# Two blocks of a transformer on one core: where low halves are kept, how head norms are summed, and the order ahead of the first expert

## The chip, the cores and the metric

The kernel runs on one core of a Trainium2 chip. The metric is the device time of one execution in microseconds (us). Engines are named as the profile names them: PE is TensorE's matmul, PEld its weight load, DVE is VectorE, ACT is ScalarE, POOL is GpSimd, SP is SyncE, which issues most of the transfers. A "q" behind an engine's name is its queue of DMA issues.

## The reference, cut to what matters

512 tokens of width 1024 (16 learned tokens are put ahead of them, 528 in all) go through two layers of a first block and one second block, all in float32.

```python
# first block, each of two layers
c_q = rmsnorm(c_q_raw, g_qa);  q = (c_q @ w_q_b).reshape(B, L, 8, 96)
k = concat([k_nope, broadcast(k_rope)]);  q, k = rmsnorm(q, g_qn), rmsnorm(k, g_kn)   # a norm per head
o = causal_block_attention(rope(q), rope(k), v)
# second block
p_diff = softmax(q1 k1) - lam * softmax(q2 k2)      # 8 heads, each with two halves of 64
merged = sigmoid(..) * attn_d + sigmoid(..) * lru_d
x = x + merged @ w_out
h2 = rms_norm(x);  logits of 4 groups and 16 experts; two experts of one group for each token
x = x + sum of silu(h2 @ w_gate) * (h2 @ w_up) @ w_down * weight
```

## The kernel before, in words

**Precision.** A large float32 product is made from three products in a rounded float32 format ("fp32r" in the trace): each operand is cast by ACT to a high half and DVE subtracts that from the original to get the low half (`split`, L139 to L147), and `mm3` (L149) adds high by high, low by high and high by low. Weights come by DMA as raw tiles of 128x1024, are split into `wh` and `wl` (L145, L146, a pool of 3), and feed `fm_steps` (L208): one step is one tile of 128 output features for all tokens, with `kt` input tiles and three matmuls for each. The steps are Python generators. Code elsewhere calls `next` on them, so that a step of matmuls stands between two steps of something that needs other engines: these are the fillers.

**Memory.** Pool `big` (L1695) has 30 slots under one tag, "A"; `pair` (L186) takes a slot for two tiles of 128x528. Tiles x2H/x2L (the normalised input of block 2), q, k, v, the gates' outputs, the heads' outputs o and the experts' raw weights all take turns in it. A tile that finds no free slot makes its writer wait for the last reader of the one whose slot it takes. Pool `med` holds smaller tiles with a few buffers to a name or a tag; tag "hl" there has two and is used, before attention 2, by the casts of LRU inputs and rope (L1022).

**Block 1, one layer** (`layer`, L378). c_kv and c_q are computed with the sums of squares on the way: ACT squares each output tile, POOL adds it up (`SquareSums.done`, L122 to L126) and `col_sums` (L370, its matmul is L374) multiplies by ones. `sums(10)` (L448) does so for c_q, whose factor `eq` is first read at L618. The inverse norm is broadcast (L452), k_rope follows (`kr` matmuls L467, `kpe` and `skr` to L490), then k and v. The q projection has six output tiles (`Q_TILES`), four for the part without rope and two for rope; `ev_q` (L531) evacuates each. The squares of q are to be summed by head: ACT makes the square (L535) and a rounded copy (L549), POOL the remainder (L550), and `q_sums` (L555, its matmul L559) multiplies both by a 0/1 table `heads` of 128x8, one tile behind. In layer 0 the tokens come in two column parts of 264, in layer 1 as one of 512. Behind it stand the z_mla steps and the k transposes (`k_steps`, L566), interleaved by hand at L599 to L622: the last `q_sums`, copies of the sums by ACT (L608), their transposes (L612), and the factor `r3q`.

**Block 2** (`block2`, L918). `attention2` (L1284) runs twice, b = 0 and 1, with four heads each. For a head, K and Q are transposed on PE (L1302) and cast by ACT (L1304). DVE makes the low halves (L1306), POOL copies halves across partitions (L1308, L1309). The tiles are KH, KL and QS, three slots of "A". KH[:, c] is the high half of K twice over, KL[:, c] its low half twice over; QS holds high and low of Q in one tile, so two matmuls of depth 128 (L1324, L1325) do what takes three otherwise. Four blocks of 128 queries follow: scores, maximum (L1326), exponential (L1328), difference, transposes (L1334), copy (L1336), product with v (L1338). After each block the generator yields, and the caller runs one filler step: for b = 1 eight steps of g_lru and then eight of g_attn (L1087 to L1096). At a head's end its output is normed, transposed (L1348) and split into a pair `o2`.

**Out of block 2 into the experts.** w_out_2 gives eight tiles `xo` (`ev_out`, L1156). Each is squared and summed, multiplied by the router's weights (`logits`, L1173), transposed into rows (`rows`, L1143) which are copied by ACT, scaled by POOL and stored to `hbuf` and `out` by SP. `finish` (logits, then rows) of a tile is held until the next tile is done; for the last, the order is sums, logits, sums, rows (L1182 to L1193). On the way SP issues loads of expert weights into slots of "A" (`prefetch`, L1110), 24 by the end. `routing` (L1398) takes a Sqrt (L1412), makes group and expert choices on DVE, ranks tokens by matmul (L1447, L1450), and `slots` (L1494) turns the ranks of some experts into a list of row numbers: a comparison `oh` on DVE for each of four token tiles (L1512), matmuls (L1507), a reduction `sl0s` (L1518). The weights' factors of the first lists follow in `factors` (L1520). `moe` (L1535) gathers an expert's 128 rows by an indirect DMA (L1550, POOL's queue), transposes them (L1560, `feature_major`), and runs gate, up and down of 16 experts; the last four of the first 28 loads go to ACT's queue (L1633).

The tile framework puts in all waits by itself and can reorder instructions of an engine within limits.

Of the kernel before, what the change touches and what calls it, by code (L numbers as in the profile page):

```python
# [20 lines left out]
P = 128  # L21
D = 1024
KD = D // P
# [111 lines left out]
class Builder:  # L135
# [107 lines left out]
    def const(self):  # L243
# [6 lines left out]
        nc.vector.memset(self.ones, 1.0)  # L250
        self.heads = cp.tile([P, len(Q_TILES), HEADS], F32R, name="heads")
        hh, lo = [cp.tile([P, len(Q_TILES), HEADS], F32, name=n) for n in ("hh", "hl")]
        for m, (rope, h) in enumerate(Q_TILES):
# [3 lines left out]
        G.tensor_scalar(hh, hh, 0.0, None, op0=ALU.is_le)  # L257
        G.tensor_tensor(self.heads, hh, lo, op=ALU.mult)
        self.fold = cp.tile([2 * ROPE, ROPE], F32, name="fold")
# [118 lines left out]
    def layer(self, l, pro, squares, w_ckv):  # L378
# [67 lines left out]
        if l == 0:  # L446
            rope_rows()
        eq = sums(10)  # L448
        V.scalar_tensor_tensor(eq, eq, 1.0 / 768, epsx, op0=ALU.mult, op1=ALU.add)
        V.tensor_scalar(eq, eq, EPS, None, op0=ALU.mult)  # L450
        inv_b = med.tile([P, T], F32, name="inv_b", bufs=1)
# [37 lines left out]
        skr = sm.tile([P, NT], F32, name="skr")  # L489
        V.tensor_reduce(skr, kpe, axis=AX.X, op=ALU.add)  # L490


# [38 lines left out]
        def ev_q(m, ps, c0, n):  # L531
            sl = slice(c0, c0 + n)
            if m not in live:
                live[m] = med.tile([P, T], F32, name="sq")
            S.activation(live[m][:, sl], ps, AF.Square)  # L535
            rope, h0 = Q_TILES[m]
            if rope:
                for i in range(4):
                    h = h0 + i
                    rows = slice(i * ROPE, (i + 1) * ROPE)  # L540
                    for f, r in enumerate((NOPE, QK)):
                        V.tensor_tensor(qT[h // 2][r:r + ROPE, h % 2, sl], ps[rows], self.TQ[f][rows, sl], op=ALU.mult)
            else:
                for e in range(2):
                    S.copy(qT[h0 // 2][:NOPE, e, sl], ps[e * NOPE:(e + 1) * NOPE])
            if c0 + n == T:
                sq = live.pop(m)[:, q0:]
                hl = [med.tile([P, T], F32R, name="z", bufs=4)[:, q0:] for w in "HL"]
                S.copy(hl[0], sq)  # L549
                nc.gpsimd.tensor_tensor(hl[1], sq, hl[0].bitcast(F32), op=ALU.subtract)  # L550
                if m:
                    q_sums(m - 1)
                live["hl", m] = hl

        def q_sums(m):  # L555
            hl = live.pop(("hl", m))
            for c, (a, w) in enumerate(q_cols):
                for i, t in enumerate(hl):
                    E.matmul(qs[c][:HEADS, :w], self.heads[:, m], t[:, a - q0:a - q0 + w],  # L559
                             start=m == 0 and i == 0, stop=m == len(Q_TILES) - 1 and i == 1)  # L560

# [38 lines left out]
        next(k_steps)  # L600
        next(z_steps)
        next(k_steps)
        q_sums(len(Q_TILES) - 1)
        sb = sm.tile([P, NT, HEADS], F32, name="sb")
        V.memset(sb[:, 0], 1.0)
        qss = med.tile([HEADS, T], F32, name="sq")
        for c, (a, m) in enumerate(q_cols):
            S.copy(qss[:, a:a + m], qs[c][:HEADS, :m])  # L608
        ps = self.psum()
        for j in q_tok:  # L610
# [9 lines left out]

        for _ in zip(z_steps, k_steps):
            pass  # L622
# [295 lines left out]
    def block2(self, xH, xL, squares, out):  # L918
# [181 lines left out]
        with ExitStack() as ctx:  # L1100
# [33 lines left out]
            for c in (0, SEQ):  # L1134
                nc.sync.dma_start(out[SEQ:SEQ + P, c:c + SEQ], zero)
            acc = self.psum()
            ssum = med.tile([P, SEQ], F32, name="ssum", bufs=1)
# [18 lines left out]
            def ev_out(m, ps, c0, n):  # L1156
# [14 lines left out]
                def logits():  # L1171
                    for j, (t0, w) in enumerate(TOK2):
                        E.matmul(acc[:, 20 * j:20 * j + 20], xo[:, t0:t0 + w], wr[:, m], start=m == 0 and j == 0,  # L1173
                                 stop=m == KD - 1, skip_group_check=True)

                def finish():
                    logits()
                    rows(m, xo)

                if m:  # L1180
                    held.pop()()
                prefetch(min(24, (11, 13, 14, 16, 18, 20, 26, 28)[m]))  # L1182
                if m < KD - 1:
                    held.append(finish)
                else:
                    square_sums(ssum)
                    logits()
                    square_sums(sq)
                    rows(m, xo)

            held = []
            self.fm(Weights(self, A["w_out_2"], 1024, 2), KD, 8, mH, mL, C0, ev_out)
            prefetch(24)  # L1193
            self.order = order
# [89 lines left out]
    def attention2(self, b, qkv, lneg, gs, out):  # L1284
# [9 lines left out]
        for hh in range(4):  # L1294
            h = 4 * b + hh
            KH = self.pair("kh2", F32R, (P, 2, SEQ))
            KL = self.pair("kl2", F32R, (P, 2, SEQ))
            QS = self.pair("q2", F32R, (P, 2, SEQ))
            for src, t2 in ((kt, KH), (qt, QS)):
                pt = self.ps_tr.tile([P, SEQ], F32, name="tr")  # L1300
                for j in range(4):
                    E.transpose(pt[:, j * P:(j + 1) * P], src[j][:, hh * P:(hh + 1) * P], self.ident)  # L1302
                for c, (own, other) in enumerate(halves):
                    S.copy(t2[own, c], pt[own])  # L1304
                    low = KL[own, c] if t2 is KH else t2[other, c]
                    V.tensor_tensor(low, pt[own], t2[own, c].bitcast(F32), op=ALU.subtract)  # L1306
                    if t2 is KH:
                        nc.gpsimd.tensor_copy(t2[other, c], t2[own, c])  # L1308
                        nc.gpsimd.tensor_copy(KL[other, c], KL[own, c])  # L1309
            po = self.ps_pv.tile([P, 4, P], F32, name="pv")  # L1310
            ot = med.tile([P, 4, P], F32, name="ot")
            so = sm.tile([P, 4], F32, name="so", bufs=2)
            for i in range(4):
# [7 lines left out]
                for c, (own, _) in enumerate(halves):  # L1321
                    c1 = slice(c, c + 1)
                    sc = self.ps_sc.tile([P, SEQ], F32, name="sc")
                    E.matmul(sc, QS[:, c, ts], KH[:, c], start=True, stop=False)  # L1324
                    E.matmul(sc, QS[:, c, ts], KL[:, c], start=False, stop=True)  # L1325
                    V.tensor_reduce(nm[:, c1], sc, axis=AX.X, op=ALU.max, negate=True)  # L1326
# [71 lines left out]
    def routing(self, acc, R):  # L1398
# [56 lines left out]
        V.tensor_tensor(rank_b.rearrange("p e j -> p j e"), ps4, ec_b, op=ALU.mult)  # L1455
        self.sl = self.slots(rank_b[:, 0:2], 2, "sl0", sm, False)
        ge, gw = sv("ge", 4, 4), sv("gw", 4)
# [23 lines left out]
        for q in range(3):  # L1481
            part = R["tok_b"][:, :, 3 + q * HX:3 + (q + 1) * HX]
            V.tensor_copy(part, fac)
            if q < 2:
                V.tensor_tensor(fac, fac, part, op=ALU.subtract)
        self.factors()
        self.cnti = sm.tile([P, 1], I32, name="cnti")
# [47 lines left out]
    def moe(self, out):  # L1535
        nc, A, tc = self.nc, self.A, self.tc
        V, S, E, G = nc.vector, nc.scalar, nc.tensor, nc.gpsimd
        with ExitStack() as ctx:
# [93 lines left out]
            W = [static_weights(e) for e in range(NE)]  # L1632
            xe = {e: gather(sl[e]) for e in range(2)}  # L1633
            for e, i in self.order[len(self.ahead):28]:
                self.ahead[e, i] = self.expert_weights(12 * e + i, queue=nc.scalar)
            x = feature_major(xe[0])
            sl += self.slots(self.rank_b[:, 2:4], 2, "sl2", self.route)
            nxt = {}
# [174 lines left out]
```

## Time and profile before

| | us |
|---|---|
| median of 3 runs (lowest, highest) | 1840.59 (1839.84, 1841.89) |
| the profiled execution | 1840.02 |
| its span in the profile | 1837.8 |
| PE busy in that span | 1742.7 (95 %) |

The span is what the profiler saw from the first to the last instruction; the execution's time has 2.2 us around it. Busy times of engines overlap. The timeline gives start and duration of instructions or of runs of equal ones ("x4" is a group of four, whose time goes from the first's start to the last's end); in square brackets stands the idle time before it and what ended it. An f32 matmul stands as two records, one of fp32r or bf16 as one. A window's line gives busy times, the mean clock granted to TensorE (1.00 is 2.4 GHz, 0.50 is 1.2 GHz), and the busy share and rate of the DMA engines.

### The profile page before, as it was taken

The page shows a single profiled execution, that of the slowest core. Times are in us where ns is not written, and L with a number is a line of the kernel's source. Part 1 is how long each engine was busy: PE and PEld are TensorE (multiplying, and loading weights), DVE is VectorE, ACT ScalarE, POOL GpSimd, SP SyncE. Part 2 cuts the span into 40 slices and gives each one's busy share as a digit, 9 for nine tenths or more (in the row PEclk, how much of TensorE's full clock was granted, in tenths as well). Part 3 has the DMA queues.
Part 4 walks back from the last instruction along what each step waited for, and adds up shares of the span by engine and source line. Part 5 has one row for each costly group of instructions (what it writes and reads, how often), then busy time and mean ns, then how long its engine had stood idle before and what let it go on. Part 6 is the DMA issues. An engine that isn't in the chain of part 4 may idle for free. (4 is left out here: it accounts for less than half of the span.)

```text
span 1837.8 us, 25780 instructions
## 1 busy us (share of the span) xinstructions
PE 1742.7 (95%) x9710; PEld 1469.6 (80%) x9710; DVE 1218.8 (66%) x2264; ACT 932.5 (51%) x1556; POOL 288.5 (16%) x261
## 2 busy tenths in 40 slices
PE   7989999999998999999998999999996997999997
PEld 7888899999976878788876777777874885888885
DVE  7575555456366455446689887577755528999996
ACT  5353244433344234433346666546645235888885
POOL 3122300001212320000213320011000031111111
PEclk9999999999999999999999999999998997999999
DMA  4222122123222122123422222122122588999992
GB/s 144 75 71 70 52 69 65 57 90 137 96 83 84 53 69 69 70 81 118 162 93 80 80 92 69 69 69 70 47 92 92 204 290 289 389 379 389 380 384 46
DMA packets 69091, 244.37 MB, mean 133 GB/s; under 512 B 10849, under 2 KB 20065, under 8 KB 57057
## 3 DMA queue, kind: packets, MB, share of 16 engines
q1 hardware_dynamic: 63776, 223.79, 33.8%
q0 software_dynamic: 4608, 16.78, 3.6%
q10 hardware_dynamic: 576, 2.10, 0.4%
q8 instruction: 78, 1.28, 0.3%
q14 instruction: 53, 0.43, 0.1%
HBM read 225.20 MB, written 17.37 MB: 132 GB/s over the span
## 5 line engine op out<-in xcount | busy, mean ns | idle before, releaser
L145 ACT CAST wh<-raw 128x1024 fp32r<-128x1024 f32 (+2 forms) x206 | 212.4, 1032 | 429.4 <-PE mm L152 358.3
L146 DVE TENSOR_TENSOR wl<-raw,wh 128x1024 fp32r<-128x1024 f32 (+2 forms) x206 | 255.0, 1239 | 107.8 <-ACT wh L145 106.3
L151 PE MATMUL mm<-xH,wh 128*128 128x264 f32 (+1 forms) x912 | 292.0, 321 | 12.9 <-ACT xH L361 8.7
L152 PE MATMUL mm<-xL,wh 128*128 128x264 f32 (+1 forms) x912 | 290.9, 320 | 0.7 <-DVE xL L362 0.7
L153 PE MATMUL mm<-xH,wl 128*128 128x264 f32 (+1 forms) x912 | 290.0, 318 | 0.0
L146 DVE TENSOR_TENSOR wl<-we,wh 128x1024 fp32r<-128x1024 f32 x192 | 227.7, 1219 | 14.9 <-ACT wh L145 12.5
L145 ACT CAST wh<-we 128x1024 fp32r<-128x1024 f32 x192 | 198.5, 1050 | 46.5 <-PE mm L153 32.0
L151 PEld LDWEIGHTS mm<-xH,wh 128*128 128x128 f32 x912 | 173.9, 191 | 25.3 <-ACT xH L361 8.7
L152 PEld LDWEIGHTS mm<-xL,wh 128*128 128x128 f32 x912 | 174.3, 191 | 11.8 <-DVE xL L362 1.5
L153 PEld LDWEIGHTS mm<-xH,wl 128*128 128x128 f32 x912 | 174.1, 191 | 10.3
L151 PE MATMUL mm<-wh,eH 128*128 128x512 f32 x256 | 104.8, 409 | 0.0
L153 PE MATMUL mm<-wh,eL 128*128 128x512 f32 x256 | 101.8, 398 | 0.0
L151 PE MATMUL mm<-x2H,wh 128*128 128x512 f32 x256 | 101.6, 397 | 0.0
L152 PE MATMUL mm<-wl,eH 128*128 128x512 f32 x256 | 101.5, 396 | 0.0
L153 PE MATMUL mm<-x2H,wl 128*128 128x512 f32 x256 | 101.0, 395 | 0.0
L152 PE MATMUL mm<-x2L,wh 128*128 128x512 f32 x256 | 100.9, 394 | 0.0
L126 POOL TENSOR_TENSOR z<-z,sq 128x528 f32<-128x528 f32 (+1 forms) x26 | 43.0, 1657 | 328.7 <-ACT sq L365 256.5
L151 PE MATMUL mm<-wh,x2H 128*128 128x512 f32 x192 | 77.3, 404 | 4.7 <-DVE rt__9409 L1264 2.7
L152 PE MATMUL mm<-wl,x2H 128*128 128x512 f32 x192 | 76.8, 400 | 0.0
L153 PE MATMUL mm<-wh,x2L 128*128 128x512 f32 x192 | 76.5, 402 | 0.0
L792 ACT ACTIVATE pr<-sc,bi,r3q 128x264 f32<-128x264 f32 (+3 forms) x80 | 46.6, 589 | 54.8 <-DVE bi L790 54.1
L152 PE MATMUL mm<-mgL,wh 128*128 128x264 f32 (+1 forms) x192 | 61.7, 321 | 0.0
(622 smaller groups left out, 4092.4 us busy)
## 6 DMA issues: line engine op xcount, KB each, us to landing
we<-in_w_moe SPq DMA_DIRECT2D x188, 512.0 KB
raw<-in_w_out SPq DMA_DIRECT2D x12, 1024.0 KB
raw<-in_w_g_mla SPq DMA_DIRECT2D x8, 1024.0 KB
raw<-in_w_g_pool SPq DMA_DIRECT2D x8, 1024.0 KB
raw<-in_w_c_q SPq DMA_DIRECT2D x6, 1024.0 KB
raw<-in_w_q_b SPq DMA_DIRECT2D x6, 768.0 KB
raw<-in_w_z_mla SPq DMA_DIRECT2D x4, 1024.0 KB
raw<-in_w_u_pool SPq DMA_DIRECT2D x4, 1024.0 KB
```

The lines of the kernel that those rows point to most:

```text
L126: self.kb.nc.gpsimd.tensor_tensor(self.sum[:, off:], self.sum[:, off:], sq[:, off:], op=ALU.add)
L145: nc.scalar.copy(H[:, :F], src)
L146: lo.tensor_tensor(L[:, :F], src, H[:, :F].bitcast(F32), op=ALU.subtract)
L151: mm(out, lH, rH, start=start, stop=False)
L152: mm(out, lH, rL, start=False, stop=False)
L153: mm(out, lL, rH, start=False, stop=stop)
L792: S.activation(pr[:, a:b, e], scs[q], AF.Exp, bias=bi[:, e:e + 1], scale=c, accum_out=su[:, e, q:q + 1])
```

## The change

1. *Low keys.* KL of attention 2 becomes two tiles of 128x512 under tag "hl" of `med`, not one slot of "A".
2. *Head sums.* `heads` becomes plain float32 and the squares of q are multiplied as they are: one f32 matmul replaces two fp32r ones, and the rounded copy and the remainder are not made.
3. *Row sums.* `sums(10)` and `eq` move behind kpe and skr. The last `q_sums` moves ahead of a k step, one z step is put between the copies and the transposes of the sums, and the rest is interleaved k first.
4. *Ahead of the first expert.* `warm` runs a Sqrt early. The last tile's logits and sums come ahead of the row copies of the last two tiles. The first list is made for expert 0 alone and its gather goes first; `factors`, the lists of experts 1 to 3 and the second gather follow. `prefetch` stops at 20, so that eight loads of the 28 go to ACT's queue, now behind `feature_major`.

```diff
@@ const, ev_q, q_sums
-        self.heads = cp.tile([P, len(Q_TILES), HEADS], F32R, name="heads")
+        self.heads = cp.tile([P, len(Q_TILES), HEADS], F32, name="heads")
...
-                live[m] = med.tile([P, T], F32, name="sq")
+                live[m] = med.tile([P, T], F32, name="z", bufs=4)
...
-                sq = live.pop(m)[:, q0:]
-                hl = [med.tile([P, T], F32R, name="z", bufs=4)[:, q0:] for w in "HL"]
-                S.copy(hl[0], sq)
-                nc.gpsimd.tensor_tensor(hl[1], sq, hl[0].bitcast(F32), op=ALU.subtract)
                 if m:
                     q_sums(m - 1)
-                live["hl", m] = hl
...
-            hl = live.pop(("hl", m))
+            sq = live.pop(m)
             for c, (a, w) in enumerate(q_cols):
-                for i, t in enumerate(hl):
-                    E.matmul(qs[c][:HEADS, :w], self.heads[:, m], t[:, a - q0:a - q0 + w],
-                             start=m == 0 and i == 0, stop=m == len(Q_TILES) - 1 and i == 1)
+                E.matmul(qs[c][:HEADS, :w], self.heads[:, m], sq[:, a:a + w], start=m == 0, stop=m == len(Q_TILES) - 1)
@@ layer
-        eq = sums(10)
-        V.scalar_tensor_tensor(eq, eq, 1.0 / 768, epsx, op0=ALU.mult, op1=ALU.add)
-        V.tensor_scalar(eq, eq, EPS, None, op0=ALU.mult)
...
         V.tensor_reduce(skr, kpe, axis=AX.X, op=ALU.add)
+        eq = sums(10)
+        V.scalar_tensor_tensor(eq, eq, 1.0 / 768, epsx, op0=ALU.mult, op1=ALU.add)
+        V.tensor_scalar(eq, eq, EPS, None, op0=ALU.mult)
...
         next(z_steps)
+        q_sums(len(Q_TILES) - 1)
         next(k_steps)
-        q_sums(len(Q_TILES) - 1)
...
             S.copy(qss[:, a:a + m], qs[c][:HEADS, :m])
+        next(z_steps)
...
-        for _ in zip(z_steps, k_steps):
+        for _ in zip(k_steps, z_steps):
+            pass
+        for _ in k_steps:
             pass
@@ attention2
-            KL = self.pair("kl2", F32R, (P, 2, SEQ))
+            KL = [med.tile([P, SEQ], F32R, name="kl2", tag="hl") for c in range(2)]
...
-                    low = KL[own, c] if t2 is KH else t2[other, c]
+                    low = KL[c][own] if t2 is KH else t2[other, c]
...
-                    E.matmul(sc, QS[:, c, ts], KL[:, c], start=False, stop=True)
+                    E.matmul(sc, QS[:, c, ts], KL[c], start=False, stop=True)
@@ block2, w_out_2
+            warm = route.tile([P, 1], F32, name="warm")
+            S.activation(warm, zero[:, :1], AF.Sqrt)
...
-                if m:
-                    held.pop()()
-                prefetch(min(24, (11, 13, 14, 16, 18, 20, 26, 28)[m]))
+                prefetch((11, 13, 14, 16, 18, 20, 20, 20)[m])
                 if m < KD - 1:
-                    held.append(finish)
+                    if m:
+                        held.pop()()
+                    held.append(lambda: (logits(), rows(m, xo)))
+                    if m == KD - 2:
+                        held[:] = [logits, partial(rows, m, xo)]
                 else:
+                    held[0]()
                     square_sums(ssum)
                     logits()
                     square_sums(sq)
+                    held[1]()
                     rows(m, xo)
...
-            prefetch(24)
@@ routing, moe
-        self.sl = self.slots(rank_b[:, 0:2], 2, "sl0", sm, False)
+        self.sl = self.slots(rank_b[:, 0:1], 1, "sl0", sm, False)
...
-        self.factors()
...
-            xe = {e: gather(sl[e]) for e in range(2)}
+            xe = {0: gather(sl[0])}
+            self.factors()
+            sl += self.slots(self.rank_b[:, 1:4], 3, "sl1", self.route)
+            xe[1] = gather(sl[1])
+            x = feature_major(xe[0])
             for e, i in self.order[len(self.ahead):28]:
                 self.ahead[e, i] = self.expert_weights(12 * e + i, queue=nc.scalar)
-            x = feature_major(xe[0])
-            sl += self.slots(self.rank_b[:, 2:4], 2, "sl2", self.route)
```

## Rows read from the trace of the kernel before

**Rows 1.** The page, part 1: the span and each engine's busy time.

```profile
span 1837.8 us, 25780 instructions
...
PE 1742.7 (95%) x9710; PEld 1469.6 (80%) x9710; DVE 1218.8 (66%) x2264; ACT 932.5 (51%) x1556; POOL 288.5 (16%) x261
```

**Rows 2.** Windows in attention 2: stretch, length, PE, PEld, DVE, ACT, POOL, clock, DMA.

```profile
1299.00:1331.00 32.00, 31.80 (x168) 25.43 (x167) 24.56 (x57) 19.48 (x44) 3.85 (x4) 1.00 0.19 66
1369.00:1411.00 42.00, 27.27 (x133) 19.05 (x132) 28.34 (x76) 23.89 (x60) 2.44 (x4) 0.88 0.08 26
1393.50:1403.80 10.30, 5.63 (x13) 3.52 (x14) 6.27 (x11) 3.60 (x8) 2.44 (x4) 0.50 0.00 0
```

**Rows 3.** The timeline from 1338 to 1370, PE and ACT, cut.

```profile
1340.39 0.58 ACT L1304 CAST kh<-tr 64x512 fp32r<-64x512 f32 x1
...
1342.49 0.63 PE L1302 MATMUL tr<-ident,qt 128*128 128x128 f32 x4
...
1368.73 0.39 PE L153 MATMUL mm<-x2H,wl 128*128 128x512 f32 x1
...
1369.30 0.58 ACT L1304 CAST q<-tr 64x512 fp32r<-64x512 f32 x1
```

**Rows 4.** The waits of PE: us in total, times, longest.

```profile
PE sc L559 <- POOL z L550: 8.0, 4, 4.3
...
PE pv L374 <- POOL z L126: 2.3, 2, 2.1
...
PE mm L612 <- ACT sq L608: 2.2, 2, 1.3
```

**Rows 5.** Windows of block 1 at the lower clock.

```profile
69.20:76.00 6.80, 6.63 (x30) 6.34 (x30) 1.96 (x10) 0.00 (x0) 0.00 (x0) 0.50 0.10 38
103.30:106.70 3.40, 3.40 (x18) 3.40 (x18) 3.09 (x11) 0.00 (x0) 0.00 (x0) 0.50 0.68 275
...
588.00:591.40 3.40, 3.40 (x9) 2.67 (x9) 2.31 (x12) 0.00 (x0) 0.00 (x0) 0.50 0.66 277
```

**Rows 6.** The timeline of PE in block 1: fp32r head sums and f32 scores.

```profile
117.94 0.65 PE L559 MATMUL sc<-z,heads 128*8 128x264 f32 x4
...
551.02 0.62 PE L559 MATMUL sc<-z,heads 128*8 128x512 f32 x2
...
649.57 1.05 PE L784 MATMUL sc<-kT,qT 128*128 128x264 f32 x4
```

**Rows 7.** The timeline from 1513 to 1533, all engines, cut.

```profile
1513.06 0.63 PE L1148 MATMUL tr<-ident,xo 128*128 128x128 f32 x4
...
1515.75 2.51 SPq L1153 DMA_DIRECT2D hbuf<-hr  x2
...
1516.55 1.28 ACT L1412 ACT_TABLE_LOAD   x1
...
1516.77 0.33 ACTq L1361 DMA_DIRECT2D we<-in_w_moe  x1
1517.85 0.26 ACT L1412 ACTIVATE v<-mm,eps 128x4 f32<-128x4 f32 x1
...
1522.85 1.43 DVE L1512 TENSOR_TENSOR oh<-iota_b,rank_b 128x256 bf16<-128x256 bf16 x4
...
1525.05 1.97 POOL L1550 DMA_INDIRECT xe<-hbuf,sl0s  x1 [7.18 <-DVE c L1469]
...
1528.86 0.51 PE L1507 MATMUL tr<-tok_b,oh 128*128 128x51 bf16 x8 [4.32 <-DVE tok_b L1483]
...
1531.64 1.73 PE L1560 MATMUL tr<-ident,xe 128*128 128x128 f32 x7 [2.27 <-DMA xe<-hbuf,sl0s]
```

**Rows 8.** Windows ahead of the first expert and within the experts.

```profile
1516.50:1531.60 15.10, 1.94 (x23) 1.34 (x22) 10.93 (x56) 4.22 (x7) 4.19 (x3) 0.50 0.99 336
1564.00:1794.00 230.00, 230.00 (x1097) 186.59 (x1096) 213.84 (x225) 196.64 (x229) 34.06 (x24) 1.00 1.03 382
```

**Rows 9.** The waits of SP's queue for a free slot: us in total, times, longest.

```profile
SPq L1361 <- DVE wl L146: 94.0, 80, 11.8
```

More of the change, by code (lines that the diff above doesn't have):

```diff
@@ L250, in const @@
         nc.vector.memset(self.ones, 1.0)
-        self.heads = cp.tile([P, len(Q_TILES), HEADS], F32R, name="heads")
-        hh, lo = [cp.tile([P, len(Q_TILES), HEADS], F32, name=n) for n in ("hh", "hl")]
+        self.heads = cp.tile([P, len(Q_TILES), HEADS], F32, name="heads")
+        hh, lo = self.heads, cp.tile([P, len(Q_TILES), HEADS], F32, name="hl")
         for m, (rope, h) in enumerate(Q_TILES):
@@ L257, in const @@
         G.tensor_scalar(hh, hh, 0.0, None, op0=ALU.is_le)
-        G.tensor_tensor(self.heads, hh, lo, op=ALU.mult)
+        G.tensor_tensor(hh, hh, lo, op=ALU.mult)
         self.fold = cp.tile([2 * ROPE, ROPE], F32, name="fold")
@@ L1174, in logits @@
                                  stop=m == KD - 1, skip_group_check=True)
-                def finish():
-                    logits()
-                    rows(m, xo)
-                if m:
-                    held.pop()()
-                prefetch(min(24, (11, 13, 14, 16, 18, 20, 26, 28)[m]))
-                if m < KD - 1:
-                    held.append(finish)
+                prefetch((11, 13, 14, 16, 18, 20, 20, 20)[m])
+                if m < KD - 1:
+                    if m:
[3 more added lines that the diff above has]
+                        held[:] = [logits, partial(rows, m, xo)]
                 else:
+                    held[0]()
                     square_sums(ssum)
@@ L1308, in attention2 @@
                         nc.gpsimd.tensor_copy(t2[other, c], t2[own, c])
-                        nc.gpsimd.tensor_copy(KL[other, c], KL[own, c])
+                        nc.gpsimd.tensor_copy(KL[c][other], low)
             po = self.ps_pv.tile([P, 4, P], F32, name="pv")
```

## The prediction

> **What bounds the kernel now.** I read the page's busy shares first. TensorE works 1742.7 us of a span of 1837.8, 95 percent, the next engine 66 percent [rows 1]. So a change that keeps the matmuls can win only what TensorE loses to waiting (some 95 us) and to its lower clock, and each edit has to be priced in the stretch where it lies. The second view was busy time by windows [rows 2]. From 1299 to 1331, while attention 2 computes two heads beside filler matmuls of the gates, TensorE works 31.80 of 32.00 us. From 1369 to 1411, where the last two heads run, it works 27.27 of 42.00, and within that, from 1393.5 to 1403.8, 5.63 of 10.30 us at a granted clock of 0.50, the lower level (1.2 GHz). The third view, the timeline of that place [rows 3], says why: the third head's K is transposed and cast by 1340.39, its Q is transposed at 1342.49, but ACT's first copy of Q starts only at 1369.30, just after the first matmul group of the last gate step ends (1368.73 plus 0.39). Between them nothing but gate matmuls run. ACT was not busy; the copy had no tile to write to. The code counts the same: pool "A" has 30 slots, and at that head 28 are taken (8 of x2H/x2L, 6 of q, k, v, 8 of the gates' output, 6 of finished heads), so KH and KL fill it and QS has to wait until the last gate step has read its x2 tile. The fillers meant for the last two heads are spent while TensorE waits for them.
>
> Fourth, the waits of TensorE [rows 4]: those that the change can touch are few, 8.0 us at L559, 2.3 at L374, 2.2 at L612. Fifth, windows behind these waits [rows 5]: four stretches at them run at 0.50, of which three are shown.
>
> **The change part by part.** Sums are made against the profiled execution, 1840.02 us (span 1837.8); the median of the runs shown, 1840.59, lies 0.57 higher, and I add that at the end.
>
> *KL in two "hl" tiles.* The third head then needs 28 + KH + QS = 30 slots, the fourth 29 + KH, and its QS takes the slot that kt leaves at the K transposes. So Q is copied behind its transposes and the gate steps spread over the heads, one beside each block. The ceiling is the idle time, 42.00 - 27.27 = 14.73 us, plus the clock's loss, half of 5.63 = 2.8: 17.5 us [rows 2]. The floor is 0, if the fillers then still run in a lump. I take 13: at the stretch's end the fourth head's own chain of softmax, transposes and output has no filler behind it. The "hl" tiles are shared with the casts before attention and turn over per head, and the next head's K low parts come well after the scores that read the last ones. That is covered by the filler beside a block; uncovered it would cost one wait of a few us a head, inside the range.
>
> *Plain f32 head sums.* Two f32r matmuls of a rounded and a remainder part become one f32 matmul, and ACT's cast and POOL's subtraction go. The 8.0 us of waits for POOL at L559 [rows 4] go with them, since ACT's square alone is then needed. The matmul costs more. Four f32r of 264 columns take 0.65, so a pair 0.33. By the records the scores at L784 are two matmuls, shown as x4: two of 264 columns take 1.05, one 0.525 [rows 6], and at 512 columns, by the columns, 1.02 against a pair's 0.62. That is +0.20 times 12 in layer 0 (six tiles, two column parts) and +0.40 times 6 in layer 1, +4.8 together; as bounds, 0 if all of it falls where TensorE idles, and 9.6 if it runs at the lower clock. I take 4.8, since TensorE is busy beside it. Two half-clock stretches of 3.40 us each (one a layer) lie at these waits, of which one stands in [rows 5]; without a stall they should run at full, which gives 1.7 each, 3.4. Net -8.0 - 3.4 + 4.8 = -6.6; range +1.6 (no clock gain, dear matmuls) to -11.4 (hidden matmuls).
>
> *Row sums moved.* The ten-column sum waits for POOL's squares, 2.3 us in two [rows 4]; behind kpe the squares are long there. After the wait TensorE runs 6.63 us at 0.50 [rows 5], of which 3.3 are loss. I take half of it, 1.7: -4.0, range 0 to -5.6. The two DVE operations on eq move with it and nothing reads eq before the keys' norms.
>
> *q_sums earlier, one z step ahead of the transposes.* L612 waits 2.2 for ACT's copies [rows 4]; the z step, matmuls of about 3.40 us of TensorE in the stretch after [rows 5], covers them. The half-clock stretch behind loses 1.7; I take half: -3.0, range 0 to -3.9.
>
> *Routing.* Here TensorE is nearly idle: 1.94 of 15.10 us from 1516.50 to 1531.60, DMA at 0.99 of its engines [rows 8]. What counts is when the gathered rows of expert 0 arrive, since from 1564 to 1794 TensorE works 230.00 of 230.00 us [rows 8], so a shift of its start carries to the end. The sums of squares now go ahead of both row copies (two groups of four transposes, 0.63 each [rows 7]), and the Sqrt's table, 1.28 us at 1516.55, is loaded long before by the warm activation. The Sqrt at 1517.85 moves some 2 us ahead; the list of one expert instead of two halves a part of the 1.43 us of "oh", so its list is there by about 1522, 3 us ahead of the gather's issue now (1525.05). But the row copies are later by the same edit: the last two hbuf stores, from 1515.75 to 1518.26, shift by about 1.5 us, and the gather reads what they wrote. So the gather can start between 1522 and 1524, and with 20 loads ahead instead of 24 fewer bytes stand in its way: xe's transposes begin now at 1531.64, 6.6 us behind the gather's issue [rows 7]. But an order stands against it: factors, which needs tok_b (the matmuls at 1528.86), and the lists of experts 1 to 3 now come ahead of expert 0's transposes. Moved 2 us ahead, those matmuls end at 1527.4 (0.51 long); the three lists, at one and a half times the width of the two now made, 1.5 times 1.43 or 2.1 us, end at 1529.5 at the earliest. In that order the transposes gain 2.1 us at most, without it up to 5. I take -3; range +1 (stores late) to -8 (all of it gained, and the gather's way shorter too).
>
> As to the table load, the row shows 1.28 us and the Sqrt 0.02 behind its end [rows 7]. The Trainium skill, "ScalarE: Activation LUTs", section What ACT_TABLE_LOAD costs, adds to a load of about 1.28 us a drain of about 1.38 for every switch of set; by it the sum would lie 1.4 us lower. The load agrees with the row, the drain isn't seen in it, and I stay with the row.
>
> *At nothing:* the casts and subtractions that go from ACT and POOL (51 and 16 percent busy [rows 1]), and the extra Sqrt load in the stage before, where TensorE's matmuls cover it.
>
> Sum: -13 - 6.6 - 4.0 - 3.0 - 3 = -29.6, so 1840.0 - 29.6 = 1810.4, and 1811 with the 0.57.
>
> **Rivals.** *The freed slot gives nothing* (0.17): the "hl" tiles turn into the new wait, or head 4's QS still waits, and the two heads stay bare. For it: buffers in this pool are all taken, so one more late release is enough. Against: the count of 30. It gives 1811 + 13 = 1824.
>
> *Small stalls only change their name* (0.08): at L559, L374 and L612 the next wait takes the place and the clock stays at 0.50 there, while f32 costs its 4.8. Then A, B and C together give +4.8 in place of -13.6: 1811 + 18.4, about 1829.
>
> *Both* (0.05): 1829 + 13 = 1842, no change.
>
> *Slower, by ACT's queue* (0.08). Eight loads instead of four are issued on ACT's queue, ahead of the next casts. On SP the same loads wait for free slots, 94.0 us in 80 waits, the longest 11.8 [rows 9]. If the slots aren't free, each of the eight holds ACT for such a wait w, and behind it queue the expert's casts, on which TensorE waits at once. Each costs w plus an issue of 0.33 [rows 7]; eight of them use up the 29.6 at w of 3.4 us. At 4.5 it is 8 times 4.83 = 38.6, and the time 1850. Against it: only 28 loads are ordered in all and the pool has 30 slots, with attention done.
>
> **How the numbers follow.** The forecast has 0.62: 1811, its own range, from the ends above, 1800 to 1823. The range goes to the second rival, 1800 to 1829, which leaves out the last two cases (0.13) and the forecast's tail. A difference of 0.2 percent, 3.7 us, is about the least that a measurement of this kernel can tell from none. Faster: 0.62 + 0.17 + 0.08 = 0.87; same 0.05; slower 0.08.
>
> **What would show it.** In the changed kernel's trace the first Q copy of the third head stands right behind its transposes, gate matmuls lie among the blocks of the last two heads, and no stretch at 0.50 is left there. L559 has 18 f32 matmuls (36 records) and no wait for POOL. No table load stands between the sums and the routing's Sqrt, and xe's transposes come some 3 us sooner after w_out_2's last matmul. The forecast is wrong if the Q copy still waits for the last gate step, if the stretches of [rows 5] stay at 0.50, or if ACT sits in front of its loads at the start of expert 0.

## The result and the profile after

The changed kernel takes 1810.75 us (median of four runs, 1807.85 to 1811.94), the kernel before in the same session 1841.24 (1839.84 to 1842.59): ratio 0.9832, interval 0.9815 to 0.9849, 30.5 us less. The forecast was 1811. The sum came out to within a microsecond, but its terms did not: several were off by 2 to 9 us, and they cancelled. That they cancelled so closely is luck. The profile of the changed kernel tells the terms apart. Its page, part 1, answers to [rows 1]: TensorE has 27 us less idle time and nearly the same work.

```profile
span 1808.2 us, 25732 instructions
...
PE 1740.5 (96%) x9706; PEld 1466.3 (81%) x9706; DVE 1215.0 (67%) x2264; ACT 925.2 (51%) x1545; POOL 264.8 (15%) x249
```

**The last two heads.** The timeline of the third head after the change, PE and ACT, answers to [rows 3].

```profile
1333.77 0.58 ACT L1302 CAST kh<-tr 64x512 fp32r<-64x512 f32 x1
...
1335.88 0.63 PE L1300 MATMUL tr<-ident,qt 128*128 128x128 f32 x4
1336.26 0.48 PE L152 MATMUL mm<-x2L,wh 128*128 128x512 f32 x1
...
1336.54 0.58 ACT L1302 CAST q<-tr 64x512 fp32r<-64x512 f32 x1 [1.44 <-PE tr L1300]
```

Q is copied 0.03 us behind its transposes (1335.88 plus 0.63), where the kernel before waited until 1369.30 [rows 3], and a gate matmul stands beside it. The whole stretch, from the K transposes of the third head to the output transposes of the fourth, as a window of the kernel before and of the one after (columns as in [rows 2]):

```profile
1331.05:1421.30 90.25, 75.03 (x358) 57.44 (x357) 48.96 (x121) 42.20 (x93) 6.85 (x17) 0.94 0.22 80
```

```profile
1324.44:1392.70 68.26, 67.92 (x352) 54.20 (x351) 48.06 (x121) 41.99 (x94) 7.90 (x17) 1.00 0.30 105
```

It is 22.0 us shorter. 14.9 of that is idle time (15.22 against 0.34). The other 7.1 lie in TensorE's own busy time, 75.03 against 67.92 for six records fewer.

**Block 1.** The waits of PE after the change, in answer to [rows 4]: L559 and L612 have none any more, L374 has one left.

```profile
PE pv L374 <- POOL z L126: 2.1, 1, 2.1
...
PE tr L1557 <- DMA xe<-hbuf,sl0s: 1.8, 1, 1.8
```

The f32 head sums in the timeline of PE, layer 0 and layer 1, in answer to [rows 6] (two records to a matmul):

```profile
101.03 1.06 PE L554 MATMUL sc<-z,heads 128*8 128x264 f32 x4
...
548.72 1.02 PE L554 MATMUL sc<-z,heads 128*8 128x512 f32 x2
```

They cost what was put in the sum: 1.06 for two of 264 columns (1.05 forecast from the scores) and 1.02 for one of 512. From the first w_q_b matmul to the first score, the windows of layer 0 and layer 1 in the kernel before, then after:

```profile
93.19:161.99 68.80, 61.79 (x486) 58.75 (x485) 50.21 (x115) 32.57 (x68) 11.62 (x6) 0.98 0.23 78
542.71:608.97 66.26, 59.10 (x264) 45.99 (x262) 42.75 (x87) 27.57 (x47) 12.66 (x6) 0.95 0.23 80
```

```profile
94.36:158.82 64.46, 63.22 (x487) 57.30 (x485) 47.04 (x115) 29.15 (x62) 0.00 (x0) 1.00 0.25 83
540.28:600.08 59.80, 59.61 (x264) 42.79 (x262) 42.16 (x87) 24.31 (x41) 0.00 (x0) 1.00 0.26 88
```

Layer 0 gives 4.34 us, layer 1 6.46, 10.8 together, and the clock, 0.98 and 0.95 before, is 1.00 in both. The row sums, on the other hand, were moved in the source, but in layer 0, where their wait is, not on the chip (in layer 1 they moved from 522.97, among the first `kr` matmuls, to 524.58, behind them). Around the sums of layer 0 the clock still falls (the first window of [rows 5]):

```profile
66.97:79.64 12.67, 10.62 (x62) 9.68 (x61) 3.68 (x14) 0.76 (x2) 2.00 (x1) 0.73 0.19 64
```

**Ahead of the first expert.** The last tile of w_out_2 is added up at 1512.45 in the kernel before:

```profile
1512.45 0.69 DVE L1160 TENSOR_TENSOR xo<-mm,xr 128x512 f32<-128x512 f32 x1 [4.76 <-PE mm L153]
```

and after the change the timeline, cut, answers to [rows 7]:

```profile
1484.82 0.69 DVE L1159 TENSOR_TENSOR xo<-mm,xr 128x512 f32<-128x512 f32 x1 [4.76 <-PE mm L153]
...
1486.33 0.63 PE L1147 MATMUL tr<-ident,xo 128*128 128x128 f32 x4
...
1487.61 0.63 PE L1147 MATMUL tr<-ident,xo 128*128 128x128 f32 x4
...
1488.08 0.95 PE L1167 MATMUL mm<-ones,sq 128*128 128x1 f32 x8
...
1489.07 0.26 ACT L1410 ACTIVATE v<-mm,eps 128x4 f32<-128x4 f32 x1 [0.16 <-PE mm L1167]
...
1496.29 1.97 POOL L1547 DMA_INDIRECT xe<-hbuf,sl0s  x1 [5.71 <-DVE c L1467]
...
1499.84 0.33 PE L1504 MATMUL tr<-tok_b,oh 128*128 128x51 bf16 x4 [4.05 <-DVE tok_b L1481]
...
1504.65 1.94 PE L1557 MATMUL tr<-ident,xe 128*128 128x128 f32 x8 [1.75 <-DMA xe<-hbuf,sl0s]
```

Counted from that addition, the Sqrt comes 4.25 us behind it (5.40 before: the table load is gone), the gather 11.47 (12.60 before), but expert 0's transposes 19.83 (19.19 before). What the earlier Sqrt gains, the gather gives back: 8.36 us from its issue to the transposes, 6.59 before [rows 7]. The shorter list itself gains nothing: from the Sqrt to the gather's issue it is 7.20 us before and 7.22 after. Its comparison `oh` takes 0.90 us instead of 1.43, but a copy ahead of it on DVE (`fac`, L1472) takes 0.81 instead of 0.16. Both groups of row transposes still stand ahead of the last sums, as before: the source says otherwise, but the framework orders each engine's instructions anew. Its order explains a second thing: all eight loads of ACT's queue are issued between 1451.94 and 1489.07, long before the experts, so the rival of a blocked ACT had nothing to stand on. The waits of SP for a slot, in answer to [rows 9]:

```profile
SPq L1359 <- DVE wl L146: 82.5, 73, 13.1
```

**The experts.** From the first expert's transposes to the end the changed kernel is shorter once more, which no step had foreseen. The transposes of successive experts in the timeline of PE of the kernel before, and after:

```profile
1593.21 1.03 PE L1560 MATMUL tr<-ident,xe 128*128 128x128 f32 x8
1612.01 1.04 PE L1560 MATMUL tr<-ident,xe 128*128 128x128 f32 x8
1630.06 1.03 PE L1560 MATMUL tr<-ident,xe 128*128 128x128 f32 x8
```

```profile
1565.54 1.03 PE L1557 MATMUL tr<-ident,xe 128*128 128x128 f32 x8
1584.15 1.03 PE L1557 MATMUL tr<-ident,xe 128*128 128x128 f32 x8
1602.05 1.03 PE L1557 MATMUL tr<-ident,xe 128*128 128x128 f32 x8
```

An expert takes 18.05 us before (1612.01 to 1630.06) and 17.90 after (1584.15 to 1602.05). One in four, with four lists made beside it, takes 18.80 and 18.61. From the first product (1533.58 and 1506.68) to the last matmul's end (1826.02 and 1796.17) that makes 292.4 and 289.5 us.

### The profile page after: what moved, and what is told of

Same layout as the page of the kernel before. It is cut to its first block, busy times and chain, and to the rows that moved or that the text cites. A ratio compares the mean times of both kernels' runs of the same rounds, so it can differ in the third digit from the quotient of the medians.

```text
span 1808.2 us, 25732 instructions
## 1 busy us (share of the span) xinstructions
PE 1740.5 (96%) x9706; PEld 1466.3 (81%) x9706; DVE 1215.0 (67%) x2264; ACT 925.2 (51%) x1545; POOL 264.8 (15%) x249
## 3 DMA queue, kind: packets, MB, share of 16 engines
q8 instruction: 78, 1.28, 0.3%
## 5 line engine op out<-in xcount | busy, mean ns | idle before, releaser
L151 PE MATMUL mm<-xH,wh 128*128 128x264 f32 (+1 forms) x912 | 292.3, 321 | 10.8 <-ACT xH L361 8.7
L152 PE MATMUL mm<-xL,wh 128*128 128x264 f32 (+1 forms) x912 | 291.4, 320 | 0.7 <-DVE xL L362 0.5
L151 PEld LDWEIGHTS mm<-xH,wh 128*128 128x128 f32 x912 | 174.7, 192 | 24.0 <-ACT xH L361 8.7
L152 PEld LDWEIGHTS mm<-xL,wh 128*128 128x128 f32 x912 | 174.4, 192 | 11.5 <-DVE xL L362 1.4
L151 PE MATMUL mm<-wh,eH 128*128 128x512 f32 x256 | 104.4, 408 | 0.0
L151 PE MATMUL mm<-x2H,wh 128*128 128x512 f32 x256 | 102.1, 399 | 0.0
L152 PE MATMUL mm<-x2L,wh 128*128 128x512 f32 x256 | 101.9, 398 | 0.0
L152 PE MATMUL mm<-wl,eH 128*128 128x512 f32 x256 | 101.0, 394 | 0.0
L151 PE MATMUL mm<-wh,x2H 128*128 128x512 f32 x192 | 77.5, 404 | 4.8 <-DVE rt__9342 L1262 2.8
L152 PE MATMUL mm<-wl,x2H 128*128 128x512 f32 x192 | 76.5, 399 | 0.0
L151 PE MATMUL mm<-mgH,wh 128*128 128x264 f32 (+1 forms) x192 | 61.7, 321 | 0.0
```

The costliest lines, as they stand in the source:

```text
L151: mm(out, lH, rH, start=start, stop=False)
L152: mm(out, lH, rL, start=False, stop=False)
```

## The experiments

**The low keys alone** (the kernel before with this edit):

```diff
-            KL = self.pair("kl2", F32R, (P, 2, SEQ))
+            KL = [med.tile([P, SEQ], F32R, name="kl2", tag="hl") for c in range(2)]
```

> Only the low keys moved into the two small tiles, all else as before. Theory: the slot decides, and alone it gives what the two traces differ by in the last two heads, 22.0 us, less 0.9 handed back in the next stage: about 1820. Rival (my forecast's own size): only the idle time and the clock inside 1369 to 1411 are won, 13 to 17.5 us: 1823 to 1828. Rival two: the gain needs the other edits too, since the framework orders everything anew: under 10 us.

Measured: 1821.47 us, ratio 0.989 (0.9874 to 0.9905), some 20 us less. The theory's number holds, and the second rival (under 10 us) falls. The interval in time ends at 1824 and so just touches the first rival (1823 to 1828); the trace settles it, since the stretch of the last two heads is 21.7 us shorter than the 90.25 before:

```profile
1333.33:1401.90 68.57, 68.23 (x354) 54.52 (x353) 48.02 (x121) 42.45 (x94) 7.90 (x17) 1.00 0.30 107
```

**All but the low keys** (the changed kernel with that edit undone):

> The changed kernel with the low keys back in a slot of the big pool. Theory: about 1811 + 21 = 1832, with the third head's Q copy again behind the last gate step. Rival: if the other edits carry the gain, it stays below 1820.

Measured: 1832.32 us, ratio 0.9951 (0.9936 to 0.9966), 21.6 above the changed kernel. Q's copy stands at 1362.01, its transposes at 1335.02. The edit is worth the same alone and on top of the others.

**29 slots:**

```diff
-            self.big = en(self.pool("big", 30, side="right"))
+            self.big = en(self.pool("big", 29, side="right"))
```

> The changed kernel with 29 slots in place of 30, the low keys still in small tiles. Theory: 28 taken + KH is 29, so the third head's Q copy waits for the gate steps once more and the gain of about 21 us goes, 1829 to 1835. Rival: if it is the low keys' place and not the count, the time stays within 4 us of 1811.

Measured: 1830.52 us, ratio 0.9936 (0.992 to 0.9951), 19.8 above the changed kernel. The third head's copies in the timeline of ACT:

```profile
1336.03 0.58 ACT L1302 CAST kh<-tr 64x512 fp32r<-64x512 f32 x1
...
1365.14 0.58 ACT L1302 CAST q<-tr 64x512 fp32r<-64x512 f32 x1
```

With the low keys in their small tiles, but one slot taken from the pool, Q waits 27 us behind its transposes (1338.14) again, and the stretch takes 90.51 us. It is the count of slots that decides, as the code's count of 28 said.

**The part ahead of the first expert alone** (warm, order of logits and rows, first list alone, 20 loads ahead, in the kernel before):

> Only the part ahead of the first expert (warm Sqrt, order of logits and rows, first list alone, 20 loads ahead). My forecast had -3 us. Theory from the two traces: the gather is issued 1.1 us sooner, its rows land no sooner because the loads of weights stand ahead of it in the DMA queues, and expert 0's transposes start within 1 us of before: 1839 to 1842. Rival: the 2.5 us that the experts are shorter in the changed kernel come from this part: 1838 or less, with experts 18.0 us apart or less.

Measured: 1838.48 us, ratio 0.9982 (0.9973 to 0.9991). Faster by 3 us, and yet not where the edits lie: from the row transposes of w_out_2's sixth tile to expert 0's it is 25.4 us in both (1506.22 to 1531.64 before, 1508.38 to 1533.76 here), and its experts stand closer:

```profile
1576.78 1.03 PE L1560 MATMUL tr<-ident,xe 128*128 128x128 f32 x8
1594.68 1.03 PE L1560 MATMUL tr<-ident,xe 128*128 128x128 f32 x8
```

The time lies between the two ranges that were expected, because a part of each came true: nothing from the routing, 17.90 us an expert. What made the experts closer was open.

**The head sums alone:**

```diff
-                for i, t in enumerate(hl):
-                    E.matmul(qs[c][:HEADS, :w], self.heads[:, m], t[:, a - q0:a - q0 + w],
+                E.matmul(qs[c][:HEADS, :w], self.heads[:, m], sq[:, a:a + w], start=m == 0, stop=m == len(Q_TILES) - 1)
```

> Only the plain f32 head sums. My forecast had -6.6 us. Theory: the four waits for POOL go and with them the half-clock stretch behind each, so from the first w_q_b matmul to the first score layer 0 gives 2 to 3 us and layer 1 some 3 to 4, 6 us together: 1835. Rival: the f32 matmuls' cost eats the gain, 1839 or more; or the whole 10.8 us that the two traces differ by in these two stretches come from here alone: 1831.

Measured: 1837.59 us, ratio 0.9974 (0.9964 to 0.9984). The two windows from w_q_b to the first score:

```profile
95.36:161.08 65.72, 63.33 (x486) 57.38 (x485) 47.42 (x115) 29.11 (x62) 0.00 (x0) 1.00 0.24 81
540.41:603.83 63.42, 61.24 (x264) 44.09 (x262) 42.44 (x87) 24.21 (x41) 0.00 (x0) 0.97 0.25 83
```

3.08 and 2.84 us less than before, 5.9 together, as the theory had it (layer 1 just under its 3 to 4). In layer 1 the clock comes back only in part with this edit alone: a wait of 2.0 us for DVE's copy of k (kT, L570) stands where the kernel before had 1.3 at L612. There a stall did change its name; in the changed kernel, with edit 3, it is gone.

**The last head sums earlier and a z step ahead of the transposes, alone:**

```diff
+        q_sums(len(Q_TILES) - 1)
         next(k_steps)
-        q_sums(len(Q_TILES) - 1)
...
+        next(z_steps)
         ps = self.psum()
```

> Only the last head sums earlier and one z step ahead of the transposes. My forecast had -3.0 us. Theory: the wait of 2.2 us at the transposes goes, with about half a stretch of lower clock: 1837 to 1839. Rival: the wait goes but the k transposes, now later, make the first scores wait: within 1 us of before.

Measured: 1838.39 us, ratio 0.998 (0.9969 to 0.999), with single runs from 1834.27 to 1842.43. The same windows:

```profile
95.67:163.06 67.39, 61.45 (x487) 58.68 (x485) 49.80 (x115) 32.63 (x68) 11.63 (x6) 0.97 0.24 79
545.38:608.26 62.88, 57.13 (x264) 44.68 (x262) 42.48 (x87) 27.72 (x47) 12.66 (x6) 0.97 0.25 84
```

1.41 and 3.38 less, 4.8 together. 5.9 and 4.8 make 10.7, and the changed kernel has 10.8: the two edits add up. With the second edit alone the wait at L612 is gone, the one at L559 stays (7.9 us).

**The experts: the tiles' place by 2 KB** (one early request of a tile in the kernel before):

```diff
             xe = {e: gather(sl[e]) for e in range(2)}
+            early = med.tile([P, 4, P], BF16, name="oh", bufs=2)
+            G.memset(early[:, 0, :1], 0.0)
```

> The kernel before with one more early buffer request in the experts' pool, so that eH, eL, hH and the lists' tiles lie at the addresses they have in the changed kernel (2 KB further on; one tiny memset is added), and no other edit. In all kernels with the edits ahead of the first expert the experts stand 17.9 us apart and without them 18.05, with the same instructions in the same order on each engine. Theory: the place of these tiles does it: 17.9 apart here as well, 1838 to 1839. Rival: it is the loads' order and queues or the lists of three: 18.05 apart, 1841 to 1842.

Measured: 1843.06 us, ratio 1.0003 (0.9994 to 1.0012). The theory, as it was put, falls: 18.06 us an expert.

```profile
1579.46 1.03 PE L1560 MATMUL tr<-ident,xe 128*128 128x128 f32 x8
1597.52 1.03 PE L1560 MATMUL tr<-ident,xe 128*128 128x128 f32 x8
```

But here the tiles were moved by 2048 bytes, and in the changed kernel, by the program's addresses, by an odd multiple of 32: warm, four bytes a partition, takes 32 in its pool and pushes all that lies behind it. So the next pair moved the tiles by 32 bytes, with one tiny copy on POOL and no other edit.

**Four bytes more in the kernel before, and four bytes more in the changed kernel:**

```diff
+            pad = route.tile([P, 1], F32, name="pad")
+            nc.gpsimd.tensor_copy(pad, zero[:, :1])
             acc = self.psum()
```

> The kernel before with one more tile of four bytes a partition in the pool of routing tiles (one tiny copy fills it), which moves eH, eL, hH, hL and every fourth wh by 32 bytes, as warm does in the changed kernel, and nothing else. Theory: it is these 32 bytes that make the matmuls of the experts closer: 17.9 us apart, the experts some 2.5 us shorter, 1839 to 1840. Rival: the loads' queues or the lists of three do it: 18.05 apart, 1842.

> The changed kernel with the same four bytes more, which puts these tiles 64 bytes, not 32, from where they were before. Theory: the experts go back to 18.05 us apart, 1813 to 1814. Rival: no change, 17.9 apart and 1811.

Measured: in the kernel before 1839.0 us, ratio 0.9985 (0.9977 to 0.9994), about 3 us faster; in the changed kernel 1814.82 us, ratio 0.9845 (0.9833 to 0.9858), 4 us slower in the median than without the pad. In the second pair the intervals overlap, and its trace has a slower start as well (last section), so the firm number is the experts' distance. Two experts each, the kernel before with the pad first, then the changed one with it:

```profile
1575.16 1.03 PE L1562 MATMUL tr<-ident,xe 128*128 128x128 f32 x8
1593.06 1.03 PE L1562 MATMUL tr<-ident,xe 128*128 128x128 f32 x8
```

```profile
1588.85 1.03 PE L1559 MATMUL tr<-ident,xe 128*128 128x128 f32 x8
1606.91 1.03 PE L1559 MATMUL tr<-ident,xe 128*128 128x128 f32 x8
```

17.90 and 18.06: the pad gives the kernel before the shorter experts and takes them from the changed one. The same two distances, to 0.02 us, part all fourteen traces: 18.05 in the six in whose programs eH lies at a multiple of 64 bytes, 17.90 in the eight where it lies 32 beyond one.

**The loads behind the first gather** (in the changed kernel):

```diff
+                            hold = xe[0] if len(parts) < 34 else None
...
+        if hold is not None:
+            self.nc.vector.tensor_copy(w[:, :1], hold[:, :1])
```

> The changed kernel with the six loads behind the 28 ordered ones held back until the first gather has landed (a one-column copy from its rows into each load's tile). Theory: the gather's rows come late because these loads stand ahead of them in the DMA queues; without them the rows are there in about 4 us after the issue instead of 8.4, and expert 0 starts up to 1.8 us sooner (TensorE's wait for the rows): about 1809. Rival: the gather takes its time for itself: no change, 1811. Third: the held loads come late for expert 1 and TensorE waits there: 1812 or more.

Measured: 1808.14 us, ratio 0.9817 (0.9803 to 0.983).

```profile
1497.79 1.97 POOL L1549 DMA_INDIRECT xe<-hbuf,sl0s  x1 [5.71 <-DVE c L1469]
...
1504.22 1.95 PE L1559 MATMUL tr<-ident,xe 128*128 128x128 f32 x8
```

From the gather's issue to the transposes 6.43 us, not 8.36, and TensorE no longer waits for the rows. By the DMA view the gather lands 5.2 us behind its issue, where it took 8.2 in the changed kernel; in five more traces with edit 4 and these loads not held it is 7.2 to 8.0, in the second one with them held (the last run below) 5.1. So the loads ahead of it did delay the gather, though the theory's 4 us was too little. The transposes now stand behind the lists of experts 1 to 3 on TensorE; 1.9 us is all that there was. In the medians this is not clear of the changed kernel's interval.

**The row sums pinned** (in the changed kernel):

```diff
-        eq = sums(10)
+        late = sm.tile([P, 1], F32, name="late")
+        V.tensor_scalar(late, skr[:, 1:2], 0.0, 1.0, op0=ALU.mult, op1=ALU.add)
+        eq = sums(10, late)
```

> The changed kernel with the ten-column sum made to stand behind skr by data (its column of ones is made from skr), since the move in the source left it in its place in layer 0, ahead of the broadcast of the inverse norm and with its wait of 2.1 us. Theory: the wait goes and part of the half-clock stretch behind it, -2 to -4: 1807 to 1809. Rival: the matmuls behind it wait for the same squares or for DVE in its place: within 1 us of 1811.

Measured: 1806.46 us, ratio 0.9807 (0.9794 to 0.9821), just under the theory's range. The place where the sum stood, in the timeline of PE of the changed kernel and of this one:

```profile
69.03 1.43 PE L374 MATMUL pv<-ones,z 128*128 128x1 f32 x10 [2.05 <-POOL z L126]
70.39 1.34 PE L346 MATMUL mm<-ident,trigq 128*128 128x128 f32 x4
```

```profile
67.67 1.04 PE L346 MATMUL mm<-ident,trigq 128*128 128x128 f32 x4 [1.31 <-DVE cqL L416]
68.64 2.17 PE L237 MATMUL mm<-ident,inv 16*128 16x16 f32 x10
```

The sum and its wait are gone from there, and a wait of 1.31 for the last c_q tile takes part of their place. From the first of the rope table's matmuls (L346, 65.16 and 64.55) to the first of the product that makes k and v (79.64 and 76.00) it is 14.48 against 11.45 us, 3.0 less. But the sum itself now stands in that product:

```profile
81.96 1.14 PE L374 MATMUL pv<-late,z 128*128 128x1 f32 x10
```

So the stage has to be taken to its end, the first w_q_b matmul (94.36 and 91.88): 29.20 against 27.33 us, 1.9 less. The medians differ by 4 us, with intervals that overlap a little; the 1.9 of the stage is the firmer number for this profile.

**Pinned and held together:**

> The pinned sum and the loads held behind the first gather together, in the changed kernel. Theory: the two lie in different stages and add up: 1.9 us from the gather and 2 to 4 from the sum, 1805 to 1807. Rival: what is won in block 1 is lost again in block 2, as some 2 us of the head sums' gain were: 1808 to 1809.

Measured: 1806.52 us, ratio 0.9806 (0.9793 to 0.9819), inside the theory's range, but no better in the median than the pinned sum alone (1806.46), so the medians do not show that the two add up. The stages do: from L346 to the first w_q_b matmul it is 25.73 us (66.49 to 92.22), 3.5 less than in the changed kernel, and from the last addition of w_out_2 to expert 0's transposes 18.16 (1480.69 to 1498.85), 1.7 less. The first differs from the 1.9 of the pinned sum alone by the clock only: from L346 to the product for k and v the granted clock was 1.00 here and 0.85 there, with the same instructions. The two kernels are the fastest of all that were run, 4 us below the changed kernel.

## Why the sum was right and its terms were not

| step | forecast | measured |
|---|---|---|
| low keys | -13 | -22.0 in the stretch |
| head sums | -6.6 | -5.9 |
| row sums moved | -4.0 | -0.3 (29.49 and 29.20 from L346 to w_q_b) |
| q_sums earlier, z step | -3.0 | -4.8 |
| routing | -3 | +0.6, inside the scatter |
| experts, 32 bytes | not foreseen | -2.9 |
| given back in block 2 | not foreseen | +2.2 ahead of the heads, +1 behind them |
| start of the program | not foreseen | +1.5 between these two profiles (L346 at 63.70 and 65.16) |
| the rest, most of it between the layers | not foreseen | +1.2 |

The measured terms add up to the difference of the two spans, 29.6 us, within rounding. Low keys, q_sums and the experts gave 13.7 more than was forecast; row sums, routing and head sums 8.0 less, and 5.9 were lost where no term stood. Nothing in the prediction made these sides meet, so the total is luck, and the mechanisms have to be judged one by one.

- **Low keys.** The mechanism held to the letter: the count of slots, Q's copy behind its transposes, the fillers beside the blocks. The rival that the freed slot gives nothing fell by the first run. The size, 13 for a measured 22.0, failed at two places. "At the stretch's end the fourth head's own chain ... has no filler behind it": only 0.34 us of idle time is left, since fillers and the first matmuls of w_attn_o were ordered into it. And the ceiling of 17.5 counted idle time and clock alone. In a bare stretch the same matmuls also stand as more busy time, since there is less to overlap; of the 7.1 us of busy time saved, 2.8 are the clock by [rows 2], about 1.4 the six records that fell behind the window (0.23 each by the distance of neighbours in the timeline, which came back as 1 us there: the output transposes are 28.6 us ahead, at 1420.64 and 1392.02, w_out_2's first matmul 27.6, at 1460.16 and 1432.52), and the rest, 2.9, is put down to this without a count of its own. (In the trace a matmul of 512 columns is 0.39 us long and the next starts 0.23 behind it; where none follows, the whole length counts.)
- **Head sums.** The mechanism was right: waits gone, matmuls at 1.02 to 1.06, clock back. The net was near, its two sides less so: with this edit alone TensorE's idle time in the two windows falls by 9.6 us (8.0 forecast) and its busy time rises by 3.7 (4.8 for the matmuls less 3.4 for the clock, 1.4, forecast).
- **Row sums.** Wrong, and for a reason that the prediction did not list: the edit did not do what it says. Moved in the source, the sum stayed in its place in layer 0. Where it was made to move, the stage gave 1.9 us with a part of the clock's loss left and 3.5 without it, against 4.0 forecast: the size was near, and the step that failed is that the move in the source was taken for one on the engine.
- **q_sums and the z step.** Right, sized too small: in layer 1 alone 3.4 us, wait and half-clock stretch together.
- **Routing.** The bound by order (a gain of 2.1 at most) was the nearer one, and even that was used up: the list won nothing, the sums did not go ahead of the row copies, and in this profile the gather lost 1.8 us behind loads in the DMA queues. The loss of 0.6 is no finding either. From the last addition to expert 0's transposes it is 19.19 to 20.26 us in six traces without edit 4 (19.19 the kernel before) and 19.00 to 19.83 in six with it and nothing held (19.83 the changed kernel). So the part is worth nothing that two profiles can tell. The Sqrt came 1.15 us sooner, which is as far as the last sums let it: they end 4.28 us behind the addition before and 4.21 after. So this move does not tell a price of 1.28 from a dearer one. The trace before does: ACT's copy ends 0.01 us ahead of the load (1515.95 plus 0.59) and the Sqrt starts 0.02 behind it [rows 7], so staying with the row was right. The Trainium skill, "ScalarE: Activation LUTs", section What ACT_TABLE_LOAD costs, has 2.66 with a drain, and no run here shows the drain.
- **What came besides.** In block 2 the first score of layer 1 is 8.9 us ahead (608.97 and 600.08), but the third group of head transposes of attention 2 only 6.7 (1128.26 and 1121.54). Part of it shows in two windows of the LRU, the kernel before and after, with the same stalls and another clock:

```profile
1010.00:1030.00 20.00, 16.73 (x66) 13.27 (x66) 19.73 (x33) 11.47 (x17) 9.52 (x8) 0.91 0.14 53
```

```profile
1002.00:1022.00 20.00, 16.91 (x62) 13.36 (x63) 19.19 (x33) 10.58 (x16) 9.33 (x7) 0.83 0.16 53
```

The slower rival, a blocked ACT, did not occur, and neither did the one in which small stalls only change their name: at L559 and L612 nothing took the place in the changed kernel.

- **The range.** The prediction says that its range, 1800 to 1823, follows from the ends of the parts. Added up, these ends are -46.4 and +2.6 us, so 1794 to 1843; the narrower range was a choice. The measured time lies in both.

## What to carry to other kernels

Count the slots of a shared pool at the point where a stall begins: one tile too many cost 20 us here, far from any engine's limit, and a run with one slot less shows it at once. A move in the source is not a move on the engine when a scheduler orders the instructions; look in the new trace where the moved one stands, and pin it by data if it has to move. And when an edit touches several stages, compare the traces stage by stage: a right total can be made of wrong terms.

## What the runs showed of the hardware that was not expected

**32 bytes.** A tile of four bytes changes the experts by 0.15 us of 18.05 (0.8 percent) each, with the same instructions in the same order on TensorE and VectorE and a granted clock of 1.00 in both. By the addresses of the programs eH, eL, hH, hL and every fourth wh lie at a multiple of 64 bytes in the slower kernels and 32 beyond one in the faster ones, while the other wh and wl lie 32 beyond one in all. Which of these tiles decides, and whether it is their place against the moving operand's, was not tried. The traces give a hint: behind an L152, whose stationary wl has the same place in all kernels and whose moving operand is eH, the next matmul starts 0.232 us later in three slower kernels and 0.230 in three faster ones (means of some 110 each), so the stationary tile's place is not all of it.

**The same stall, three clocks.** From 32 to 44 us, behind a stall of 1.9 to 2.1 us (L151 waits for `cqL`) that these kernels share, the granted clock was 1.00, 0.86 or 0.72, in the kernel before, the one with the low keys alone and the changed one with the pad in turn:

```profile
32.00:44.00 12.00, 10.09 (x85) 9.98 (x84) 9.04 (x42) 4.54 (x10) 2.08 (x1) 1.00 0.04 14
```

```profile
32.00:44.00 12.00, 10.13 (x73) 10.03 (x72) 8.33 (x39) 4.05 (x10) 2.09 (x1) 0.86 0.05 14
```

```profile
32.00:44.00 12.00, 9.87 (x62) 9.77 (x62) 8.10 (x45) 4.19 (x10) 0.00 (x0) 0.72 0.05 14
```

The edit of the second kernel lies in attention 2, a thousand microseconds later, so it is not the cause; the changed kernel has 0.86 here too, and 1.00 with the sums pinned. It is worth 1 to 3 us (10 to 23 matmul records fewer in the window, at 0.12 us each), so a difference of that size between two profiles says nothing until the stage it lies in is known.
